# A turned tile stored in four scattered pieces and loaded whole, in a one-core transformer block

## The chip, the cores and the metric

The kernel runs on one core of a Trainium2 chip. The core has a matrix engine (TensorE, PE in the profile, with its weight loads as PEld), a vector engine (DVE), a scalar engine (ACT), a general engine (POOL), a queue engine (SP) and 16 DMA engines that move data between DRAM and the on-chip memory of 128 partitions (SBUF). The metric is the time of one launch in device microseconds, lower being better; the median of several runs is compared.

## The reference

One block over 256 tokens of width 2048, in float32: a gated FFN of width 5632, a mixer of two branches (a state-space scan, S5, and a gated spatial unit, SGU), and a second gated FFN, each with an RMS norm ahead and a residual around it.

```python
def swiglu_ffn(h, w_gate, w_up, w_down):
    return (jax.nn.silu(h @ w_gate) * (h @ w_up)) @ w_down

h = rms_norm(x, ffn1_norm[i])
x = x + 0.5 * swiglu_ffn(h, ffn1_w_gate[i], ffn1_w_up[i], ffn1_w_down[i])
h = rms_norm(x, mix_norm[i])
proj = h @ w_in[i]
y_a = s5_mixer(proj[..., :S5_WIDTH], ...)
y_b = sgu_mixer(proj[..., S5_WIDTH:], ...)
g_a, g_b = jnp.split(jax.nn.sigmoid(h @ w_gate[i] + b_gate[i]), 2, axis=-1)
x = x + (g_a * (y_a @ w_branch_a[i]) + g_b * (y_b @ w_branch_b[i])) @ w_out[i]
h = rms_norm(x, ffn2_norm[i])
x = x + 0.5 * swiglu_ffn(h, ffn2_w_gate[i], ffn2_w_up[i], ffn2_w_down[i])
return rms_norm(x, final_norm)
```

## The kernel before, in words

**Products.** Each weight and each activation is split into a high and a low part, and a product is three matmuls: high by high, high by low, low by high. `job` (L222) computes 256 tokens by 512 output columns: it runs `step` (L214) over the inner dimension in blocks of 128, six matmuls of 128x512 in each (three for either half of the tokens). The chunks of 128x2048 weights stand in one list in the order of their use. SP loads a chunk into `raw` (three buffers); ACT writes its high part `whi` (L148) and DVE its low part `wlo` (L149), three buffers of each; a chunk serves four steps. `take` (L195) calls `tick` (L176) once a step, and at a chunk's first step the chunk two further on is split. So the split of a chunk waits until TensorE is done with the one three before it.

**The order of the other work.** Every engine works in the order in which its instructions were written. Work that isn't matmuls is hung on ticks: `pend` holds what a finished product still needs and runs at the next tick, `at(n, fn)` runs fn n ticks later, and `fillers` are generators of which a step is run at some of the ticks. In the first FFN the filler is `s5_prepare` (L383), which computes the tables of S5, with many small transfers on POOL's queue and its arithmetic on DVE: `eb` and `bt` are loaded (L563, L565) and multiplied (L402), `ca` is stored as `stash_c` (L588) before the next `ca` is written.

**The FFN.** `ffn` (L331) runs in three groups of 4, 4 and 3 blocks of 512 hidden columns. For each block one job makes the gate product (`gate_evac`, SiLU into a tile `t`), one the up product (`up_evac`, L340, which multiplies into `t`, L347). The result lies tokens by columns and is wanted columns by tokens, split into high and low, in `gt`, for the down products after the group. Two ways lead there. The last block of a group is turned by TensorE, two ticks on (`turned`, L254: transposes `q`, L260, between the matmuls). The others, 3 + 3 + 2 in each FFN and 16 in all, go by `turned_dma` (L263): DVE transposes 32x32 blocks within 32 partitions (L266) into another buffer of `t`, POOL's queue carries the blocks to their places by way of a DRAM tile `turn`, into `w`, and 26 ticks after the call ACT and DVE split `w` into `gt` (L246, L247). `t` and `turn` have two buffers each, `w` one.

**POOL's queue.** POOL issues all of these transfers and the S5 ones, in the order written. A transfer that reads what another wrote is issued only when that one has landed, and POOL waits for it, so that all behind it on POOL waits too.

Of the kernel before, what the change touches and what calls it, by code (L numbers as in the profile page):

```python
# [9 lines left out]
F32 = mybir.dt.float32  # L10
# [8 lines left out]
P = 128  # L19
# [6 lines left out]
N = 512  # L26
# [24 lines left out]
def kernel(  # L51
# [31 lines left out]
    act, dve, pe, pool = nc.scalar, nc.vector, nc.tensor, nc.gpsimd  # L83
# [5 lines left out]
    dr = ctx.enter_context(tc.tile_pool(name="dr", bufs=1, space=DRAM))  # L89
# [79 lines left out]
    def at(delta, fn):  # L169
        hooks.setdefault(st["tick"] + delta, []).append(fn)  # L170
# [68 lines left out]
    def tmp():  # L239
        return ev.tile([P, 2, N], F32, tag="t", name="t", bufs=2)  # L240
# [22 lines left out]
    def turned_dma(src, pl, put, wait):  # L263
        tt = tmp()
        for h in range(2):
            dve.transpose(out=tt[:, h, :], in_=src[:, h, :])  # L266
        d = dr.tile([P, 2, N], F32, tag="turn", name="turn", bufs=2)
        pool.dma_start(out=d, in_=tt)  # L268
        dv = d.rearrange("(a j) h (k b i) -> a b j (h k) i", a=4, b=4, k=4)
        w = pl.tile([P, 2, 4, P], F32, tag="tw", name="w")  # L270
        for a in range(4):
            pool.dma_start(out=w.rearrange("p h k (a i) -> p a (h k) i", a=4)[:, a], in_=dv[a])  # L272

        def arrived():
            for h in range(2):
                put(slice(h * P, h * P + P), w[:, h])
        at(wait, arrived)
# [53 lines left out]
    def ffn(hT, gp, last_down, begin=None, rates=None):  # L331
# [8 lines left out]
        def up_evac(gt, j, n):  # L340
            def put(b, q):
                split2(gt[:, 4 * j + 2 * b:4 * j + 2 * b + 2], q)

            def evac(acc):
                s = state["g"]
                for h in range(2):
                    dve.scalar_tensor_tensor(out=s[:, h, :], in0=acc[:, h, :], scalar=rc(h), in1=s[:, h, :],  # L347
                                             op0=ALU.mult, op1=ALU.mult)
                if j < n - 1:
                    turned_dma(s, gp, lambda c, w: split2(gt[:, 4 * j:4 * j + 4], w, c), 26)  # L350
                else:
                    at(2, lambda: turned(s, 0, put))
            return evac
# [852 lines left out]
```

## Time and profile before

| what | value |
|---|---|
| median of 3 runs | 2039.59 us |
| lowest and highest | 2035.46 and 2049.26 us |
| the profiled execution | 2037.03 us |
| its span, first to last instruction | 2035.1 us |
| mean granted TensorE clock | 0.996 |
| busy: PE, DVE, ACT, POOL | 2010.9, 1146.0, 864.8, 216.8 us |
| POOL, 64 loads w<-turn (L272) | 134.5 us busy |
| POOL, 16 stores turn<-t (L268) | 9.3 us busy |
| DMA queue of SP, share of 16 engines | 56.6% |
| DMA queue of POOL, share of 16 engines | 10.1% |

A group of instructions is named by its line, engine, operation and what it writes and reads (`w<-turn`). In a timeline each row has the start in us from the span's beginning, how long the row's instructions took, engine, line, operation, tiles and count, and in brackets how long the engine had been idle and what ended that. For a transfer the time in the row is that of its issue; "DMA to landing" is the time from the issue until its data have arrived (least, median and most of the transfers asked for). In a list of waits stand the waiting engine and line, whom it waited for, the total in us, how often, and the longest.

### The profile page before, as it was taken

The numbers are of one execution on the slowest core, as the hardware profiler recorded it, in microseconds if no ns is written. First come the engines' busy times: TensorE is split into PE (matmuls) and PEld (weight loads), VectorE is DVE, ScalarE is ACT, GpSimd is POOL, SyncE is SP. The second block draws the span as 40 slices with busy tenths as digits, with TensorE's granted clock in tenths as the row PEclk, the third lists the DMA queues.
The fourth block names the chain that finished last, engine by engine and source line by source line (L and its number), as shares of the span: only waits on it lengthen the run. The fifth ranks groups of instructions, "written<-read, shape, count | busy, mean of one in ns | idle before, by whom it ended". The sixth has DMA issues, their size and how long they took to land.

```text
span 2035.1 us, 23133 instructions
## 1 busy us (share of the span) xinstructions
PE 2010.9 (99%) x9636; PEld 1662.4 (82%) x9636; DVE 1146.0 (56%) x1138; ACT 864.8 (42%) x709; POOL 216.8 (11%) x214
## 2 busy tenths in 40 slices
PE   9999999999999999989999999999999999999998
PEld 7887888887888888878888988888888888888886
DVE  5775565666664555546775565545554445544454
ACT  7543334444333455434345444443433343333343
POOL 0131002332012000010100000011100121000200
PEclk9999999999999999999999999999999999999999
DMA  8888678886668655547755544578855688555873
GB/s 313 223 230 220 241 233 226 234 236 200 218 211 223 195 197 196 204 171 263 242 198 209 205 175 177 180 211 216 224 201 191 201 208 224 199 198 203 212 214 124
DMA packets 78008, 429.75 MB, mean 211 GB/s; under 512 B 17696, under 2 KB 18352, under 8 KB 32080
## 3 DMA queue, kind: packets, MB, share of 16 engines
q1 hardware_dynamic: 53280, 378.56, 56.6%
q0 software_dynamic: 22176, 45.50, 10.1%
q10 hardware_dynamic: 2448, 4.22, 0.6%
q8 instruction: 75, 1.23, 0.3%
q14 instruction: 29, 0.24, 0.0%
HBM read 406.60 MB, written 20.84 MB: 210 GB/s over the span
## 4 chain that ended last, share of the span: by engine, by line
PE 90%; DMA 4%; issue 2%; DVE 1%; POOL 1%; ACT 1%; SPq 0%; ACTq 0%; POOLq 0%; DVEq 0%
PE acc L218 29%; PE acc L219 28%; PE acc L220 28%; DMA bt<-in_s5bt_dram 1%; PE q L260 1%; DMA raw<-in_w1s_dram 1%; DMA stash_c<-ca 1%; POOL w L272 1%; DMA raw<-in_w1u_dram 1%; DVE wlo L149 1%; ACT whi L148 1%; DMA stash_g<-gsb 0%; PE acc L236 0%; PE acc L235 0%; PE q L745 0%
## 5 line engine op out<-in xcount | busy, mean ns | idle before, releaser
L149 DVE TENSOR_TENSOR wlo<-raw,whi 128x2048 fp32r<-128x2048 f32 (+1 forms) x363 | 815.3, 2248 | 777.4 <-ACT whi L148 777.4
L148 ACT ACTIVATE whi<-raw 128x2048 fp32r<-128x2048 f32 (+1 forms) x363 | 682.6, 1882 | 916.9 <-PE acc L220 760.9
L218 PE MATMUL acc<-whi,h 128*128 128x512 f32 x1856 | 726.1, 391 | 0.9 <-ACT whi L148 0.9
L219 PE MATMUL acc<-wlo,h 128*128 128x512 f32 x1856 | 723.1, 390 | 1.2 <-DVE wlo L149 1.2
L220 PE MATMUL acc<-whi,h 128*128 128x512 f32 x1856 | 722.8, 389 | 0.0
L218 PEld LDWEIGHTS acc<-whi,h 128*128 128x128 f32 x1856 | 348.8, 188 | 74.1 <-ACT whi L148 1.3
L219 PEld LDWEIGHTS acc<-wlo,h 128*128 128x128 f32 x1856 | 348.8, 188 | 73.9 <-DVE wlo L149 2.3
L220 PEld LDWEIGHTS acc<-whi,h 128*128 128x128 f32 x1856 | 348.6, 188 | 72.8
L218 PE MATMUL acc<-whi,gt 128*128 128x512 f32 x680 | 266.9, 392 | 0.0
L219 PE MATMUL acc<-wlo,gt 128*128 128x512 f32 x680 | 265.6, 391 | 0.0
L220 PE MATMUL acc<-whi,gt 128*128 128x512 f32 x680 | 265.4, 390 | 0.0
L220 PEld LDWEIGHTS acc<-whi,gt 128*128 128x128 f32 x680 | 127.8, 188 | 27.6
L218 PEld LDWEIGHTS acc<-whi,gt 128*128 128x128 f32 x680 | 127.9, 188 | 27.1
L219 PEld LDWEIGHTS acc<-wlo,gt 128*128 128x128 f32 x680 | 127.9, 188 | 26.7
L272 POOL DMA_DIRECT2D w<-turn x64 | 134.5, 2105 | 134.3 <-issue 84.0
L268 POOL DMA_DIRECT2D turn<-t x16 | 9.3, 583 | 860.2 <-DVE t L266 860.2
L337 ACT ACTIVATE t<-acc,rc 128x512 f32<-128x512 f32 x44 | 27.9, 686 | 63.4 <-PE acc L220 63.4
L218 PE MATMUL acc<-whi,mT 128*128 128x512 f32 x128 | 50.2, 392 | 0.0
L220 PE MATMUL acc<-whi,mT 128*128 128x512 f32 x128 | 49.9, 389 | 0.0
L219 PE MATMUL acc<-wlo,mT 128*128 128x512 f32 x128 | 49.8, 389 | 0.0
L312 DVE SCALAR_TENSOR_TENSOR x_sb<-acc,x_sb 128x1024 f32<-128x1024 f32 x27 | 33.1, 1224 | 29.7 <-PE acc L220 29.7
L291 ACT ACTIVATE junk<-x_sb 128x512 bf16<-128x512 f32 x32 | 20.2, 631 | 57.2 <-DVE x_sb L312 51.9
(205 smaller groups left out, 1113.4 us busy)
## 6 DMA issues: line engine op xcount, KB each, us to landing
raw<-in_w1d_dram SPq DMA_DIRECT2D x44, 1024.0 KB, 5.1
raw<-in_w2g_dram SPq DMA_DIRECT2D x44, 1024.0 KB, 4.9
raw<-in_w2u_dram SPq DMA_DIRECT2D x44, 1024.0 KB, 5.3
raw<-in_w2d_dram SPq DMA_DIRECT2D x44, 1024.0 KB, 4.8
raw<-in_w1g_dram SPq DMA_DIRECT2D x40, 1024.0 KB, 5.7
raw<-in_w1u_dram SPq DMA_DIRECT2D x40, 1024.0 KB, 5.9
raw<-in_w_in_dram SPq DMA_DIRECT2D x24, 1024.0 KB, 4.8
raw<-in_w_gb_dram SPq DMA_DIRECT2D x16, 1024.0 KB, 5.0
```

The costliest lines, as they stand in the source:

```text
L148: act.activation(out=hi[:, s], in_=r[:, s], func=AF.Copy)
L149: dve.tensor_tensor(out=lo[:, s], in0=r[:, s], in1=f(hi[:, s]), op=ALU.subtract)
L218: pe.matmul(acc[:, h, :], lhsT=lhs[:, k, 0, t], rhs=hi, start=first, stop=False)
L219: pe.matmul(acc[:, h, :], lhsT=lhs[:, k, 0, t], rhs=lo, start=False, stop=False)
L220: pe.matmul(acc[:, h, :], lhsT=lhs[:, k, 1, t], rhs=hi, start=False, stop=last)
L260: pe.transpose(q[:, i, h * P:h * P + P], src[:, h, c:c + P], ident)
L268: pool.dma_start(out=d, in_=tt)
L272: pool.dma_start(out=w.rearrange("p h k (a i) -> p a (h k) i", a=4)[:, a], in_=dv[a])
L291: act.activation(out=j, in_=x_sb[:, h, m * N:m * N + N], func=AF.Square, accum_out=ssq[:, h, m:m + 1])
L312: dve.scalar_tensor_tensor(out=xs, in0=acc, scalar=scale, in1=xs, op0=ALU.mult, op1=ALU.add)
L337: act.activation(out=s[:, h, :], in_=acc[:, h, :], func=AF.Silu, scale=rc(h))
```

## The change

The rearrangement moves from the loads to the stores. Before, one store writes the transposed tile to DRAM as it lies, 128 rows of 4 KB, and four loads, one for each block of 32 rows, each fetch 1024 pieces of 128 bytes (32 numbers) and put them into all 128 partitions. After it, four stores, one for each 32 partitions of the tile, write 1024 pieces of 128 bytes each to their places in DRAM, and one load fetches 128 rows of 4 KB as they lie. `turn` has another shape and the same size; what arrives in `w` is the same.

```diff
         for h in range(2):
             dve.transpose(out=tt[:, h, :], in_=src[:, h, :])
-        d = dr.tile([P, 2, N], F32, tag="turn", name="turn", bufs=2)
-        pool.dma_start(out=d, in_=tt)
-        dv = d.rearrange("(a j) h (k b i) -> a b j (h k) i", a=4, b=4, k=4)
+        d = dr.tile([4, 32, 2, 4, P], F32, tag="turn", name="turn", bufs=2)
+        dv = d.rearrange("b j h k (a i) -> a j (h k) b i", a=4)
+        for a in range(4):
+            pool.dma_start(out=dv[a], in_=tt[32 * a:32 * a + 32].rearrange("j h (k b i) -> j (h k) b i", k=4, b=4))
         w = pl.tile([P, 2, 4, P], F32, tag="tw", name="w")
-        for a in range(4):
-            pool.dma_start(out=w.rearrange("p h k (a i) -> p a (h k) i", a=4)[:, a], in_=dv[a])
+        pool.dma_start(out=w.rearrange("p h k t -> p (h k t)"), in_=d.rearrange("b j h k t -> (b j) (h k t)"))
```

Only POOL's instructions differ. The first place is POOL at the third call, which stands at 143 us in the profile, with the loads of `eb` and `bt` behind it. In brackets are the counters that a row waits for: DVE_49 and Activation_49 count what DVE and ACT have done, DMASW0 to DMASW7 the landings of POOL's transfers, which take the eight counters in turn. Before:

```order
L268 DMA turn_1199<-t_1196 128x1024 [waits DMASW1_49,DVE_49]
L272 DMA w_1201<-turn_1199 128x8x32 [waits DMASW3_49,DMASW2_49,DMASW4_49,DMASW1_49,Activation_49]
L272 DMA w_1201<-turn_1199 128x8x32 x2
L272 DMA w_1201<-turn_1199 128x8x32 [waits DMASW5_49]
L563 DMA eb_1306<-stash_e_84 128x1x512 [waits DMASW7_49,DMASW6_49,DVE_49]
L563 DMA eb_1306<-stash_e_84 128x1x512 [waits DMASW0_49]
L565 DMA bt_1309<-in_s5bt_dram 128x2x512
```

And the same place on POOL after the change:

```order
L270 DMA turn_1199<-t_1196 256x4x32 [waits DVE_49]
L270 DMA turn_1199<-t_1196 256x4x32 x2
L270 DMA turn_1199<-t_1196 256x4x32 [waits DMASW4_49]
L272 DMA w_1204<-turn_1199 128x1024 [waits DMASW3_49,DMASW4_49,DMASW2_49,DMASW5_49,DMASW1_49,Activation_49]
L563 DMA eb_1306<-stash_e_84 128x1x512 [waits DMASW7_49,DMASW6_49,DVE_49]
L563 DMA eb_1306<-stash_e_84 128x1x512 [waits DMASW0_49]
L565 DMA bt_1309<-in_s5bt_dram 128x2x512
```

The wait for landed stores (counters 1 to 4) has moved from the second of the five transfers to the last, right ahead of `eb` and `bt`, and now stands for four stores instead of one.

The second place is POOL at the sixth call, at 419 us in the profile, with the store of `ca` and the small transfers of `gsb` behind it, as the difference between the two programs:

```order
 L622 DMA stash_t<-tt 128x512
 L556 DMA par<-in_s5bc_dram 128x4x128
-L268 DMA turn<-t 128x1024
-L272 DMA w<-turn 128x8x32 x4
+L270 DMA turn<-t 256x4x32 x4
+L272 DMA w<-turn 128x1024
 L588 DMA stash_c<-ca 128x1280
 L614 DMA stash_g<-gsb 16x1024
```

`stash_c` stood behind the issue of four loads and now stands behind the landing of four stores.

## The prediction

> **What bounds the kernel now.** I read the engines' shares first, then TensorE's waits, then a table of stretches cut where TensorE is idle, and last the timelines of POOL, DVE and ACT there. The columns of the stretches are: bounds, length, then the busy time (instructions) of PE, PEld, DVE, ACT and POOL, the granted clock, the DMA share and GB/s.
>
> ```profile
> PE q L260 <- DVE t L347: 5.3, 4, 3.9
> 180.00:196.00 16.00, 11.88 (x50) 9.51 (x49) 11.62 (x14) 4.09 (x5) 1.78 (x3) 0.89 0.55 194
> 196.00:456.00 260.00, 260.00 (x1209) 213.51 (x1208) 152.18 (x124) 109.18 (x91) 51.07 (x57) 1.00 0.79 233
> 456.00:470.00 14.00, 12.83 (x60) 10.22 (x59) 11.36 (x13) 5.47 (x5) 5.35 (x10) 1.00 0.64 202
> 864.00:885.00 21.00, 15.19 (x64) 12.26 (x63) 7.47 (x14) 4.98 (x4) 1.46 (x2) 0.84 0.33 119
> 885.00:2026.00 1141.00, 1140.23 (x5699) 945.78 (x5697) 618.31 (x439) 470.77 (x355) 95.74 (x83) 1.00 0.65 204
> 140.34 0.39 PE L219 MATMUL acc<-wlo,h 128*128 128x512 f32 x1
> 140.56 0.39 PE L220 MATMUL acc<-whi,h 128*128 128x512 f32 x1
> ```
>
> TensorE is the bound almost everywhere: from 196 to 456 us it has no idle time, from 885 to 2026 it has 0.8 us, although half of the 16 turned tiles pass there. It is idle in three places in mid program: 16.00 - 11.88 = 4.1 us near 186, 1.2 us near 462, and 5.8 us near 867, where no turned tile is under way. At the first the granted clock is 0.89 over 16 us, another 16 x 0.11 = 1.8 us. So the change can give back at most 4.1 + 1.8 + 1.2 = 7.1 us of 2035, and can cost time wherever it lets TensorE wait. Matmuls start 0.22 to 0.23 us apart (140.34, 140.56), so a weight chunk of 24 matmuls takes 24 x 0.226 = 5.4 us.
>
> **The change, part by part.** Before, a turned tile leaves as one store, and four loads fetch it. The rows are from the call at 1351.84, where nothing else uses POOL; the landing lines belong to the first and the fourth load, and the last row is ACT reading the tile.
>
> ```profile
> 1351.84 0.60 POOL L268 DMA_DIRECT2D turn<-t  x1 [270.66 <-DVE t L266]
> 1355.49 6.36 POOL L272 DMA_DIRECT2D w<-turn  x3 [3.04 <-DMA turn<-t]
> 1366.65 2.09 POOL L272 DMA_DIRECT2D w<-turn  x1 [4.80 <-issue]
> ...
> DMA to landing us min/median/max: 10.8/10.8/10.8
> ...
> DMA to landing us min/median/max: 16.4/16.4/16.4
> ...
> 1384.96 1.14 ACT L246 ACTIVATE gt<-w 128x512 fp32r<-128x512 f32 x2
> 1387.01 1.92 ACT L148 ACTIVATE whi<-raw 128x2048 fp32r<-128x2048 f32 x1 [0.91 <-PE acc L220]
> ```
>
> The four loads need 1366.65 + 16.4 - 1355.49 = 27.6 us, that is 6.9 us each, though POOL spends 2.1 us on each; the fourth is issued 0.4 us after the first has landed (1355.49 + 10.8 = 1366.3). The tile is complete 31.2 us after the store was issued, and is read at 33.1: 1.9 us to spare.
>
> Removed: the wide store, 0.6 us of POOL and 3.6 us until the first load starts. Added: four stores, each of 1024 pieces of 128 bytes, as many and as long as a load had, but written to DRAM in pieces where the loads read DRAM in pieces. POOL writes out as many pieces as before, so I take 2.1 us for each issue, beside other work. Their time to landing is the one unknown price. The nearest rows are the loads (same pieces, other direction) and the four stash_e stores of 32 KB, 128 pieces of 256 bytes each (same direction), which stood right behind a load:
>
> ```profile
> 118.23 2.10 POOL L272 DMA_DIRECT2D w<-turn  x1 [6.78 <-issue]
> 124.24 2.22 POOL L512 DMA_DIRECT2D stash_e<-em  x4 [3.91 <-DVE em L402]
> ...
> DMA to landing us min/median/max: 14.5/14.5/14.5
> ...
> DMA to landing us min/median/max: 9.2/9.2/9.3
> ```
>
> The first landing line is the load's, the second that of the small stores. The load landed at 118.23 + 14.5 = 132.7, the first small store at 124.24 + 9.2 = 133.4, the fourth, issued about 125.9, at 135.2. So 384 pieces took 1.8 us, about POOL's own pace of issue (0.56 us each): at most 4.8 us for 1024 pieces. Lower end of the price: POOL's 2.1 us for each store. Upper end: twice the loads' 6.9 us, since nothing in the trace writes 128-byte pieces. I take the loads' price, 27.6 us for four: the piece size and the count are the same, and the written row stands below it, not above.
>
> The Trainium skill speaks against the change here ("DMA: Bandwidth & Descriptors", Specifications): below 512 bytes a transfer falls short of line rate because the DMA engine reads, modifies and writes. By that rule as it stands stores and loads of 128 bytes are both slow, and the sum stays; taken as a rule for DRAM writes alone, it leads to the last rival below. The stash_e rows, at 256 bytes, show no such charge.
>
> Added too: one wide load, 512 KB in rows of 4 KB, which waits on POOL for all four stores. Loads of that size:
>
> ```profile
> vt<-stash_v POOLq DMA_DIRECT2D x4, 512.0 KB, 6.0
> tab<-stash_w POOLq DMA_DIRECT2D x4, 512.0 KB, 4.9
> ```
>
> So 5 to 6 us. The tile is then complete 27.6 + 0.4 + 5.5 = 33.5 us after the first store is issued, against 31.2: 0.4 us after ACT's usual 33.1. What covers it: the split that follows stands until 1387.01 for TensorE's release, 0.9 us after the reads end, and weights are split two chunks ahead, 10.8 us less 1.9 (ACT) and 2.3 (DVE) for the split, 6.6 us. A tile may be 7.5 us late before TensorE runs dry. Price of the later tile: 0. Without that cover each of the 16 calls would cost what exceeds it.
>
> The stage buffer t is held for 28 us instead of 3; its buffer is next written by the next call's transpose, two jobs of 16 steps on, 2 x 16 x 6 x 0.226 = 43 us. Price 0.
>
> The rest is what stands behind the call in POOL's queue, and only in the first FFN, where the preparation of the S5 tables runs beside it. Before, POOL was free once the fourth load was issued, and what followed queued in the DMA engines; now POOL itself stands until the stores have landed.
>
> ```profile
> 143.20 0.58 POOL L268 DMA_DIRECT2D turn<-t  x1 [16.74 <-DVE t L266]
> 146.79 6.31 POOL L272 DMA_DIRECT2D w<-turn  x3 [3.01 <-DMA turn<-t]
> 158.33 2.10 POOL L272 DMA_DIRECT2D w<-turn  x1 [5.24 <-issue]
> 160.43 1.21 POOL L563 DMA_DIRECT2D eb<-stash_e  x2
> 161.62 0.76 POOL L565 DMA_DIRECT2D bt<-in_s5bt_dram  x1
> 194.22 0.58 POOL L573 DMA_DIRECT2D stash_v<-vt  x1 [31.84 <-DVE vt L402]
> 196.02 0.77 POOL L565 DMA_DIRECT2D bt<-in_s5bt_dram  x1
> ...
> DMA to landing us min/median/max: 16.8/16.8/16.8
> ...
> DMA to landing us min/median/max: 9.8/9.8/9.8
> ...
> 184.25 1.29 DVE L402 TENSOR_TENSOR m<-eb,bt 128x512 f32<-128x512 f32 x2 [3.43 <-DMA bt<-in_s5bt_dram]
> 189.00 1.40 DVE L347 SCALAR_TENSOR_TENSOR t<-acc,rc,t 128x512 f32<-128x512 f32 x2
> ```
>
> Place one, the call at 143.20. The landing lines are those of the fourth load and of the second bt. The first bt landed at 184.2, as DVE's wait shows; DVE stood 3.4 us for it, the gate product t came late, and TensorE waited at its transposes (q): the 4.1 us. Now: four loads ran from 146.79 to 158.33 + 16.8 = 175.1, 28.3 us, so the stores land at 143.2 + 28.3 = 171.5; the wide load is issued at 171.9, eb and bt follow until 174.5. The same four sizes in a row were issued from 194.22, and the last, bt, landed at 196.02 + 9.8 = 205.8, 11.6 us on. So bt lands at 171.9 + 11.6 = 183.5: 0.7 us earlier. Term: -0.7 us. Bounds: -3.4 and the clock's 1.8 if the stores are cheaper, +2 if the wide load is the slower kind.
>
> ```profile
> 419.24 0.55 POOL L268 DMA_DIRECT2D turn<-t  x1
> 424.56 6.33 POOL L272 DMA_DIRECT2D w<-turn  x3 [4.76 <-DMA turn<-t]
> 438.86 2.09 POOL L272 DMA_DIRECT2D w<-turn  x1 [7.98 <-issue]
> 440.94 0.60 POOL L588 DMA_DIRECT2D stash_c<-ca  x1
> ...
> DMA to landing us min/median/max: 14.6/14.6/14.6
> ...
> DMA to landing us min/median/max: 15.6/15.6/15.6
> ...
> DMA to landing us min/median/max: 4.8/4.8/4.8
> ...
> 456.59 0.83 DVE L402 TENSOR_TENSOR ca<-m,m 128x640 f32<-128x640 f32 x1 [1.04 <-DMA stash_c<-ca]
> ```
>
> Place two, the call at 419.24. The landing lines are those of the fourth load, of stash_c and of the 512 KB store at 194.22. DVE overwrites ca only when stash_c has landed (440.94 + 15.6 = 456.5), and the next t follows: TensorE's 1.2 us. The loads took 438.86 + 14.6 - 424.56 = 28.9 us, and their first waited 4.8 us for a store that elsewhere took 3.0, so I add 1.7 for what lies ahead in the queue: stores landed at 419.24 + 28.9 + 1.7 = 449.8, wide load issued at 450.2, stash_c right behind it. At 194.22 the first 512 KB landed in 4.8 us and the next 1024 KB by 11.6, 6.8 us; 640 KB behind 512 KB take 4.8 + 6.8 x 640/1024 = 9.1 us, so stash_c lands at 450.2 + 9.1 = 459.3: +2.8 us. The call before it, at 372, ends its chain of small POOL transfers later in the same way, and this call follows that chain without a gap: +1.0 us, between 0 and 2.5. A wait grown from 1.2 to 5.0 us may also lower the clock as at 186: 0 to 1.8 us; I take 0.
>
> Sum: -0.7 + 2.8 + 1.0 = +3.1 us. The profiled execution took 2037.03 us (span 2035.1), so 2040.1, in round numbers 2040. It lay 2.6 us below the median 2039.59, so the same sum beside the median is 2042.7.
>
> **Rivals.**
> *The stores are cheaper than the loads.* The stash_e rows speak for it, with 4.8 us or less for 1024 pieces; against it, those were few, and of 256 bytes. Four stores then land after 19 us or less, bt and stash_c come over 8 us earlier, and both waits go: 3.4 + 1.8 + 1.0 = 6.2 us less, 2031. It can give no more, as TensorE is busy elsewhere.
>
> *The stores are dearer, and TensorE waits at every tile.* Mechanism: writes of 128 bytes to DRAM land later than reads, the wide load goes out later, and ACT, which works in order, stands at gt<-w ahead of the weight splits. It decides from 33.1 + 7.5 = 40.6 us after the first store on, that is when four stores take over 40.6 - 5.9 = 34.7 us, 1.26 times the loads. At 1.5 times (41.4 us) a call is 47.3 - 40.6 = 6.7 us too late, 16 calls 107 us, and with a lowered clock of up to 1.8 us at each 136: 2144 to 2173. At twice the price (55.2 us) 20.5 us a call, 328 us: 2365 or more. Against it: the stash_e rows. By the Trainium skill's rule above, read as one for DRAM writes alone, this is the case that comes, and 2365 stands against the 2040 by the rows.
>
> *It only trades places.* The same pieces cross the same DMA engines; 3.6 us before the loads become 5.9 us behind the stores, and both POOL places stay as they are: 2037. This lies within the forecast's own bounds.
>
> **How the numbers follow.** Forecast (loads' price, trading places with it): 0.56, its own range 2034 to 2046 by the bounds above. Cheaper stores: 0.24, 2029 to 2033. Dearer: 0.20, of which only a twentieth part lies below 2058, just past the tipping point. The range 2029 to 2058 then holds about 0.8. A measurement of this kernel tells about 1%, 20 us, from no change. Faster by that much is beyond the 7.1 us there are: 0.03 for what I have not seen. Slower by over 1%: nearly all of the dearer case, 0.19. Within 1%: 0.78.
>
> **What would show it.** In the profile after: L270 with 64 issues of about 2.1 us, the fourth of each call waiting for the first to land; L272 16 times, about 0.6 us, idle before it some 14 to 18 us for turn<-t. Landing of turn<-t near 10.8 to 16.4 us, as for the loads, says the price is right; under 6 us is the cheap case, over 21 the dear one. ACT gt<-w waiting for w about 0.5 us a call is the forecast; more than 7 us is the rival, and TensorE then has idle time after 1340. Near 186 the wait should stand at about 3.4 us and near 462 at some 5.0. I am wrong if weight loads land so late beside the stores that ACT waits for raw more than now and TensorE with it.

## The result and the profile after

| | before | after |
|---|---|---|
| median, 9 runs each | 2039.59 us | 2028.99 us |
| lowest and highest | 2034.53 and 2049.26 | 2028.22 and 2029.78 |
| profiled execution (span) | 2037.03 (2035.1) | 2029.23 (2027.3) |

After / before is 0.9946, with a 95% interval of 0.9931 to 0.9961: 10.6 us less, half a per cent. The runs also lie closer together: 1.6 us from lowest to highest instead of 14.7. The forecast was 2040 in a range of 2029 to 2058, so the median lies 0.01 us below its low end, and the sign of the movement was the other one.

From the page after: busy time by engine, packets, the queues of SP (q1) and POOL (q0), the shares of the chain that ended last, and the group of the scattering stores (busy us, mean ns, idle time before).

```profile
PE 2008.8 (99%) x9636; PEld 1660.9 (82%) x9636; DVE 1145.8 (57%) x1138; ACT 864.4 (43%) x709; POOL 144.9 (7%) x214
...
DMA packets 71865, 428.97 MB, mean 212 GB/s; under 512 B 11552, under 2 KB 12208, under 8 KB 25936
...
q1 hardware_dynamic: 53280, 378.56, 52.8%
q0 software_dynamic: 16032, 44.71, 7.7%
...
PE 97%; DVE 1%; DMA 1%; ACT 1%; issue 1%; SPq 0%; ACTq 0%
...
L270 POOL DMA_DIRECT2D turn<-t x64 | 63.5, 999 | 931.2 <-DVE t L266 931.2
```

The same lines of the page before:

```profile
DMA packets 78008, 429.75 MB, mean 211 GB/s; under 512 B 17696, under 2 KB 18352, under 8 KB 32080
...
q0 software_dynamic: 22176, 45.50, 10.1%
...
PE 90%; DMA 4%; issue 2%; DVE 1%; POOL 1%; ACT 1%; SPq 0%; ACTq 0%; POOLq 0%; DVEq 0%
```

POOL is busy 72 us less, and 1.0 us with each store where each load cost 2.1. The bytes are nearly the same, but POOL's queue has 22176 - 16032 = 6144 packets fewer, all of them small: 96 for each of the 64 loads that are gone. TensorE makes up 97% of the chain that ended last, where it was 90%.

TensorE's waits after (total us, times, longest), the two largest beside one of 1.4 us at the start of the program:

```profile
PE q L260 <- DVE u_all L934: 4.6, 1, 4.6
...
PE q L907 <- DVE u_all L934: 1.2, 1, 1.2
```

Both stood there before too, near 867. The waits for `t` (L347), 5.3 us in all before, are gone. The stretches after, with the columns of the prediction's table:

```profile
180.00:196.00 16.00, 16.00 (x76) 13.25 (x75) 11.58 (x11) 5.95 (x5) 2.57 (x4) 1.00 0.68 207
...
456.00:470.00 14.00, 14.00 (x67) 11.55 (x66) 9.42 (x12) 6.46 (x8) 0.00 (x0) 1.00 0.64 236
```

TensorE is busy without a gap at both places, at full clock. That is 4.1 us of idle time and 1.7 us of clock near 186, and 1.2 us near 462: 7.0 of the 7.8 us between the two spans.

How this comes about is seen at the third call. The timelines of POOL and of DVE after:

```profile
142.48 3.95 POOL L270 DMA_DIRECT2D turn<-t  x4 [16.14 <-DVE t L266]
153.40 0.56 POOL L272 DMA_DIRECT2D w<-turn  x1 [6.97 <-DMA turn<-t]
153.95 1.25 POOL L563 DMA_DIRECT2D eb<-stash_e  x2
155.19 0.76 POOL L565 DMA_DIRECT2D bt<-in_s5bt_dram  x1
...
177.57 1.28 DVE L402 TENSOR_TENSOR m<-eb,bt 128x512 f32<-128x512 f32 x2
...
183.13 1.40 DVE L347 SCALAR_TENSOR_TENSOR t<-acc,rc,t 128x512 f32<-128x512 f32 x2
```

And how long these transfers took from issue to landing (least, median, most), first the stores of this call, then its `bt`:

```profile
DMA to landing us min/median/max: 3.3/6.5/7.6
...
DMA to landing us min/median/max: 10.6/10.6/10.6
```

The four stores are issued 1 us apart, and POOL goes on 10.9 us after the first (153.40 - 142.48). The loads had taken 28 us here. `bt` lands at 155.19 + 10.6 = 165.8 instead of 184.2, 12 us before DVE comes to it, and `t` starts at 183.13 instead of 189.00. By page and timeline, then, four stores are far cheaper than the four loads they replace. What makes them so, and why that is worth microseconds at one call and nothing at others, the experiments ask.

### The profile page after: what moved, and what is told of

The parts are those of the page before. It is cut to its first block, busy times and chain, and to the rows that moved or that the text cites. A ratio compares the mean times of both kernels' runs of the same rounds, so it can differ in the third digit from the quotient of the medians.

```text
span 2027.3 us, 23118 instructions
## 1 busy us (share of the span) xinstructions
PE 2008.8 (99%) x9636; PEld 1660.9 (82%) x9636; DVE 1145.8 (57%) x1138; ACT 864.4 (43%) x709; POOL 144.9 (7%) x214
## 3 DMA queue, kind: packets, MB, share of 16 engines
q0 software_dynamic: 16032, 44.71, 7.7%
## 4 chain that ended last, share of the span: by engine, by line
PE 97%; DVE 1%; DMA 1%; ACT 1%; issue 1%; SPq 0%; ACTq 0%
PE acc L218 31%; PE acc L220 31%; PE acc L219 31%; PE q L260 1%; DMA raw<-in_w1s_dram 1%; ACT whi L148 0%; DVE wlo L149 0%; PE q L609 0%; PE acc L236 0%; PE acc L235 0%; PE acc L234 0%; PE q L745 0%; PE q L702 0%; DVE r L671 0%; PE acc L1099 0%
## 5 line engine op out<-in xcount | busy, mean ns | idle before, releaser
L270 POOL DMA_DIRECT2D turn<-t x64 | 63.5, 999 | 931.2 <-DVE t L266 931.2
L291 ACT ACTIVATE junk<-x_sb 128x512 bf16<-128x512 f32 x32 | 20.2, 630 | 56.9 <-DVE x_sb L312 51.6
L347 DVE SCALAR_TENSOR_TENSOR t<-acc,rc,t 128x512 f32<-128x512 f32 x44 | 30.9, 745 | 16.8 <-PE acc L220 16.8
```

Source lines behind the costliest of these rows:

```text
L270: pool.dma_start(out=dv[a], in_=tt[32 * a:32 * a + 32].rearrange("j h (k b i) -> j (h k) b i", k=4, b=4))
L291: act.activation(out=j, in_=x_sb[:, h, m * N:m * N + N], func=AF.Square, accum_out=ssq[:, h, m:m + 1])
```

## The experiments

These were the theories after the result. On the price: *direction* (pieces of 128 bytes are dear to fetch from DRAM and cheap to put there); *form* (the loads were dear by the shape of their access pattern). Each of the old loads runs over 128 partitions and, in DRAM, over a pattern whose first dimension is 4 (`b`); each new store takes 32 partitions, and its first dimension in DRAM is 32 (`j`) as the kernel writes it. (The program folds this 32 and the 8 behind it, which lie evenly, into one of 256: hence the `256x4x32` in its rows. The 4 of the old loads stays a 4 there.) On the gain: *place one*, by `bt`, by the tile `w` or by the weights coming late there; against it, a gain all over, from less traffic.

### Gathering again, in the stores' form

One wide store and four gathering loads, as before, but each load takes 32 partitions and begins with a dimension of 32 in DRAM.

```diff
-        dv = d.rearrange("(a j) h (k b i) -> a b j (h k) i", a=4, b=4, k=4)
+        dv = d.rearrange("(a j) h (k b i) -> b j (h k) a i", a=4, b=4, k=4)
...
-        for a in range(4):
-            pool.dma_start(out=w.rearrange("p h k (a i) -> p a (h k) i", a=4)[:, a], in_=dv[a])
+        for b in range(4):
+            pool.dma_start(out=w[32 * b:32 * b + 32].rearrange("j h k (a i) -> j (h k) a i", a=4), in_=dv[b])
```

> The wide store as before, and four gathering loads with the access pattern of the changed kernel's stores turned round: each load fills 32 partitions with 1024 pieces of 128 bytes. Theory direction (reading DRAM in small pieces is dear, writing it is not): the four loads take 25 to 29 us as before, the tile is complete about 31 us after the store, TensorE waits about 4 us near 186 us and about 1 us near 462, and the time is 2036 to 2043 us. Theory form (the pattern over 128 partitions with an outermost dimension of 4 is dear, in either direction): POOL spends 1.0 us instead of 2.1 on each load, the four take about 10 us, the tile is complete about 14 to 16 us after the store, neither wait is left, and the time is 2028 to 2031 us.

Measured: 2029.4 us, ratio to before 0.9956 (0.994 to 0.9971), as the theory of the form has it. The view of transfers (count, KB each, median us from issue to landing) of this kernel:

```profile
w<-turn POOLq DMA_DIRECT2D x64, 128.0 KB, 5.8
```

and of the kernel before:

```profile
w<-turn POOLq DMA_DIRECT2D x64, 128.0 KB, 14.8
```

Loads of the same bytes in the same number of 128-byte pieces, from the same kind of DRAM tile, land in 5.8 us instead of 14.8, and the whole gain is there. The direction is not the cause.

### Scattering, in the old loads' form

The changed kernel, its four stores each over 128 partitions, with a first dimension of 4 in DRAM: the mirror of the old loads.

```diff
-        dv = d.rearrange("b j h k (a i) -> a j (h k) b i", a=4)
-        for a in range(4):
-            pool.dma_start(out=dv[a], in_=tt[32 * a:32 * a + 32].rearrange("j h (k b i) -> j (h k) b i", k=4, b=4))
+        dv = d.rearrange("b j h k (a i) -> b a j (h k) i", a=4)
+        for b in range(4):
+            pool.dma_start(out=dv[b], in_=tt.rearrange("p h (k b i) -> p b (h k) i", k=4, b=4)[:, b])
```

> Four scattering stores and one wide load as in the changed kernel, but each store takes 1024 pieces of 128 bytes from all 128 partitions, with the access pattern of the loads before turned round (outermost dimension 4 on the DRAM side). Theory direction: POOL about 1 us for each store, the four land within about 10 us, 2028 to 2031 us. Theory form: POOL 2.1 us for each store, the fourth waits for the first to land, the four land after 25 to 29 us, the tile is complete after 31 to 35 us, and the time is 2036 to 2046 us.

Measured: 2034.07 us, ratio 0.9975 (0.9959 to 0.9991); the profiled run took 2040.84. Its transfers, and below its wait for `t`:

```profile
turn<-t POOLq DMA_DIRECT2D x64, 128.0 KB, 14.4
```

```profile
PE q L260 <- DVE t L347: 9.7, 4, 7.5
```

The stores are now as dear as the loads were, POOL's issue costs 131.5 us for the 64, and the 6144 small packets are back (17697 under 512 bytes). In this execution TensorE waits for `t` again. The form costs the same in both directions.

The time itself missed the 2036 to 2046 that was expected for the form: the median lies 5 us below the 2039.16 of before beside it. The twelve runs go from 2029.96, as fast as the changed kernel, to 2040.84, which is the one profiled. So the price of the transfers is shown, but how much of it reaches the time differs from run to run, and why it is less in most runs here stays open.

### 128 partitions without the dimension of 4

Does a transfer suffer from spanning all 128 partitions, or from the 4? Here the tile passes by four stores in the cheap form and four loads of 128 partitions each whose first dimension in DRAM is 128 too, once with the pieces 256 bytes apart and once adjacent.

```diff
+        d = dr.tile([4, 4, 32, 8, 64], F32, tag="turn", name="turn", bufs=2)
...
+            pool.dma_start(out=d[a].rearrange("b j k i -> j k b i")[:, :, :, 0:32],
+                           in_=tt[32 * a:32 * a + 32].rearrange("j h (k b i) -> j (h k) b i", k=4, b=4))
...
+            pool.dma_start(out=w.rearrange("p h k (a i) -> p a (h k) i", a=4)[:, a],
+                           in_=d[a].rearrange("b j k i -> (b j) k i")[:, :, 0:32])
```

> Both sides rearranged, to take the pattern of the loads before apart: four cheap scattering stores as in the changed kernel, then four loads of 1024 pieces of 128 bytes over all 128 partitions, whose DRAM side has no outermost dimension of 4 any more, but pieces 256 bytes apart, so that neither side of a load is whole. Theory outermost 4 (that dimension made the loads before dear): 1.0 us of POOL for each load and about 10 us for the four. Theory whole side (a transfer is cheap when one of its sides is in whole rows, because only the other is then cut into pieces): 2.1 us of POOL each, the fourth waits for the first to land, and 24 to 29 us for the four.

> The same with the DRAM pieces next to each other, so that a load's DRAM side is whole and its SBUF side is 1024 pieces over 128 partitions. Both theories: about 1.0 to 1.3 us of POOL for each load and about 10 us for the four. If they take 24 to 29 us here too, both fall, and it is the 128 partitions with eight pieces each that are dear.

Measured, one run each: 2028.83 and 2029.14 us. The loads with the pieces apart:

```profile
w<-turn POOLq DMA_DIRECT2D x64, 128.0 KB, 6.4
```

128 partitions alone don't make a load dear. All forms side by side (busy us of POOL for the 64 transfers, median us to landing; the first dimension as the kernel writes it, the program folds 32 to 256 and 128 to 1024):

| transfers | first dimension in DRAM, partitions | POOL | landing |
|---|---|---|---|
| loads, before | 4, 128 | 134.5 | 14.8 |
| stores of the second experiment | 4, 128 | 131.5 | 14.4 |
| stores, after | 32, 32 | 63.5 | 5.8 |
| loads of the first experiment | 32, 32 | 62.9 | 5.8 |
| loads of the third, apart | 128, 128 | 56.8 | 6.4 |
| loads of the third, adjacent | 128, 128 | 56.9 | 6.7 |

The dear ones are those with the 4 in front. No run has a 4 in front over 32 partitions, or another small number there, so how the price goes with that number isn't measured. The Trainium skill has a rule of this form ("DMA: Bandwidth & Descriptors", in the section on why a DMA increments its semaphore by 16 and not by 1): a transfer is spread over the largest number of DMA engines, up to 16, that divides the first dimension above 1 of both sides. By it the dear forms ran on 4 engines and the others on 16. All six rows agree with it, also with the folded dimensions; that only 4 engines were at work the trace doesn't show, since it names no engine for a packet, and neither does it say what the 96 extra packets are.

### Where in the program the gain arises

The changed form in some of the calls only; the others keep the old one.

```diff
+        n = turns[0]
+        turns[0] += 1
+        if n == 2:
...
```

The condition is `n >= 8` for the second FFN, `n == 2` for the third call (place one), `3 <= n <= 5` for calls 4 to 6 (place two among them).

> The changed form in the eight calls of the second FFN, the form before in the eight of the first. Theory queue (what counts is how long the S5 transfers behind a turned tile on POOL's queue are held up, which is so in the first FFN alone): no gain, 2036 to 2041 us, with TensorE's waits near 186 and 462 us still there. Rival, weights (the pieces hold up the weight loads in every call, and a part of a microsecond is won at each): half of the gain, about 2033 to 2035 us.

> The changed form in the third call alone (place one), the form before in the other 15. Theory places (the gain is what the waits near 186 and 462 us cost, and the first belongs to the third call): the wait near 186 and the lowered clock behind it are gone, the wait near 462 stays at 1 to 3 us, and the time is 2029 to 2033 us, most of the whole gain. Rival, stretch (the pieces of every call of the first FFN crowd the DMA engines, and each adds a share): a sixth to a third of the gain, 2036 to 2038 us.

> The changed form in the fourth, fifth and sixth call (place two), the form before elsewhere. Theory places: the wait near 462 is gone, that near 186 stays, with its changing size from run to run, and the time is 2035 to 2039 us, 1 to 4 us below before. Rival, stretch: half of the gain, 2032 to 2035 us.

| changed form in | median us | before beside it | ratio (95%) |
|---|---|---|---|
| the second FFN, 8 calls | 2039.68 | 2039.16 | 1.001 (0.9996 to 1.0025) |
| the third call alone | 2030.94 | 2039.23 | 0.9962 (0.9948 to 0.9976) |
| calls 4 to 6 | 2038.46 | 2039.23 | 0.9996 (0.9982 to 1.001) |

The third call alone brings 8.3 us, about four fifths of the gain. Eight calls of the second FFN bring nothing, and calls 4 to 6 nothing that can be told from nothing, though near 462 TensorE no longer waits there. So it is not a gain from less traffic: it arises where a late transfer reaches TensorE. The third call and calls 4 to 6 together make 9.1 of the 10.6 us; the rest is less than these intervals can tell, and the other calls of the first FFN had no run of their own.

The profile of the second-FFN kernel, whose first FFN is the old one, also shows that place one differs from run to run. Its wait:

```profile
PE q L260 <- DVE t L359: 9.4, 2, 9.3
```

There DVE went on with `bt` at 189.13, and TensorE's longest wait for `t` was 9.3 us, against 3.9 in the profiled execution of before.

### What is late at place one: bt moved out of POOL's queue

The kernel before, with `eb` and `bt` of the first group issued by ACT, so that they don't stand behind the gathering loads.

```diff
+            q = act if g == 0 else pool
...
-                pool.dma_start(out=eb[:, i, :], in_=se[i, :, gw].unsqueeze(1).to_broadcast([8, 16, GP * 64]))
+                q.dma_start(out=eb[:, i, :], in_=se[i, :, gw].unsqueeze(1).to_broadcast([8, 16, GP * 64]))
...
-            pool.dma_start(out=bt, in_=s5bt[:, :, gw])
+            q.dma_start(out=bt, in_=s5bt[:, :, gw])
```

> The turned tiles as before; only the loads of eb and bt of the first of the four S5 groups are issued from ACT's queue instead of POOL's, so that they no longer stand behind the four gathering loads of the third call. Theory queue: bt lands well before DVE wants it at 181 us, TensorE's wait of about 4 us near 186 and the lowered clock behind it are gone, the wait near 462 stays, and the time is 2029 to 2034 us. Rival, weights: the wait near 186 comes from the traffic of the pieces itself, and the time stays at 2036 to 2041 us.

Measured: 2037.23 us, ratio 0.9994 (0.9978 to 1.0009). Of that kernel the waits of ACT for weights from 150 to 200 us:

```profile
ACT whi L148 <- DMA raw<-in_w1u_dram: 7.0, 1, 7.0
...
ACT whi L148 <- DMA raw<-in_w1d_dram: 4.0, 1, 4.0
```

ACT's waits for weights in the kernel before, from 140 to 200 us (the changed kernel has none there):

```profile
ACT whi L148 <- DMA raw<-in_w1d_dram: 5.9, 2, 5.8
...
ACT whi L148 <- DMA raw<-in_w1u_dram: 3.2, 1, 3.2
```

And DVE's timeline with `bt` on ACT's queue:

```profile
181.04 1.29 DVE L247 TENSOR_TENSOR gt<-w,gt 128x512 fp32r<-128x512 f32 x2
182.25 1.29 DVE L402 TENSOR_TENSOR m<-eb,bt 128x512 f32<-128x512 f32 x2
...
186.99 1.40 DVE L347 SCALAR_TENSOR_TENSOR t<-acc,rc,t 128x512 f32<-128x512 f32 x2
```

DVE comes to `bt` without waiting, and yet `t` starts at 186.99, 3.9 us later than in the changed kernel, and TensorE waits 2.5 us. Now the weights are late: ACT stood 7.0 and 4.0 us for `raw`, so that it came to the tile `w` only at 178.71, when that had landed (157.96 + 19.2 = 177.2), and DVE split it at 181.04 instead of 176.36. Before, ACT had stood 9.1 us for `raw` here too, but `bt` came later still. The expectation that `bt` is the whole of it was missed. Since `bt`, the weights and the tile can each be late here, two more runs hold back one alone.

### One transfer late at a time

First a run that did not do what it was meant to: in the changed kernel `eb` and `bt` of the first group stand four steps later in the program.

```diff
+             early = 4 if g == 0 else 0
+             for _ in range(early):
+                 yield
...
```

> The changed kernel, with the loads of eb and bt of the first S5 group issued about 18 us later (four of the five filler steps between them and their use now stand ahead of them). The turned tile's pieces are then long through, so the DMA engines are no more crowded than in the changed kernel, and only bt is late, as it was before. Theory bt (DVE, which works in order, stands for bt, and TensorE for what DVE has behind it): DVE waits 3 to 6 us for bt, TensorE 3 to 6 us near 186 with a lowered clock behind it, 2033 to 2038 us. Rival, crowding (the wait before came from weights and tile held up on the DMA engines, bt's lateness being a bystander): no wait near 186, 2028 to 2030 us.

Measured: 2029.51 us, ratio 0.9948 (0.9933 to 0.9963). `bt` was issued at 154.51, no later than in the changed kernel (155.19): POOL has no work between, and its order alone does not hold a transfer back. The run tells nothing about a late `bt`.

So POOL was held by a chain of small copies between a scratch tile and DRAM, each waiting for the last. Seven of them ahead of `eb` and `bt` make only these late; six of them, behind `bt` and ahead of the wide load, make only the tile late. Both are the changed kernel otherwise, but for DVE filling the scratch tile once. The first of the two edits:

```diff
+            if g == 0:
...
+                for n in range(7):
+                    pool.dma_start(**(dict(out=ht, in_=hd) if n % 2 else dict(out=hd, in_=ht)))
```

> Changed kernel; in the third call seven small copies of 16 KB, each waiting for the one before, stand on POOL between the wide load and the eb and bt loads of the first group, so that bt alone is late and nothing crowds the transfers. By the spacing of the stores in the changed kernel (about 3 us from issue to landing) they hold POOL some 18 us: bt should land near 182 to 187 instead of 165.8 (184.2 before). Theory A (bt's lateness made the wait near 186): DVE waits for bt for 3 us or more, TensorE waits for t L347 near 186 again, and 3 to 8 us of the gain are lost: 2032 to 2037. Theory B (the crowding of the tile and the weights made it): DVE may wait for bt, but it catches up, and the time stays at 2028 to 2031.

> Changed kernel; in the third call the eb and bt loads are issued ahead of the wide load, and six small copies between them hold the wide load some 15 us, so that the turned tile w alone is late: it should land near 175 to 180 instead of 157.5 (175.1 before), and bt earlier than 165. Theory B1 (the late tile holds DVE up): DVE or ACT waits for w at the tile's four products and TensorE waits for t L347 near 186: 2031 to 2034. Theory B2 (the weight loads' lateness, not the tile's): no wait of TensorE near 186, 2028 to 2030.

Measured: with `bt` late 2041.11 us, ratio 1.0008 (0.9991 to 1.0024); with the tile late 2036.94 us, ratio 0.998 (0.9962 to 0.9998). DVE's timeline with `bt` late:

```profile
176.00 1.29 DVE L247 TENSOR_TENSOR gt<-w,gt 128x512 fp32r<-128x512 f32 x2
188.81 1.29 DVE L402 TENSOR_TENSOR m<-eb,bt 128x512 f32<-128x512 f32 x2 [11.51 <-DMA bt<-in_s5bt_dram]
...
193.55 1.40 DVE L347 SCALAR_TENSOR_TENSOR t<-acc,rc,t 128x512 f32<-128x512 f32 x2
```

and with the tile late:

```profile
182.98 1.29 DVE L247 TENSOR_TENSOR gt<-w,gt 128x512 fp32r<-128x512 f32 x2 [6.82 <-ACT gt L246]
184.19 1.28 DVE L409 TENSOR_TENSOR m<-eb,bt 128x512 f32<-128x512 f32 x2
...
188.92 1.40 DVE L354 SCALAR_TENSOR_TENSOR t<-acc,rc,t 128x512 f32<-128x512 f32 x2
```

`bt` alone late gives the whole gain back, and the tile alone late some 8 of the 10.6 us, while ACT waits for no weights from 150 to 200 us in either. Both took longer than was expected (2032 to 2037 and 2031 to 2034): the copies held more back than the kernel before did, `bt` to 188.8 instead of 184.2 and the tile to 177.02 + 5.3 = 182.3 instead of 175.1. So the runs show what a late `bt` or tile does, not the size of either in the kernel before, where the tile landed 2.1 us ahead of ACT's reading it (177.20). The theory that DVE would catch up with a late `bt` is refuted, and so is the one that only the weights' lateness counts. Whichever is late, it holds DVE, which works in order, ahead of `t`. Put together, the start of `t` (L347; the line moves with the edits), what held DVE before it, and TensorE's longest wait for it in the profiled run of each kernel:

| kernel | what is late | t starts at | TensorE waits |
|---|---|---|---|
| after | nothing | 183.13 | 0 |
| bt issued by ACT | weights | 186.99 | 2.5 |
| tile held | tile | 188.92 | 4.2 |
| before | weights, then bt | 189.00 | 3.9 |
| calls 4 to 6 only | weights, then bt | 189.04 | 4.4 |
| scattering in the old form | weights and tile, then bt | 192.06 | 7.5 |
| bt held | bt | 193.55 | 8.9 |
| second FFN only | weights and tile, then bt | 193.87 | 9.3 |

Start less wait lies between 184.5 and 185.1 in all that wait. That is the point from which it costs: in the changed kernel `t` has some 1.4 us to spare (184.5 - 183.13), and in these runs every microsecond beyond is paid in full.

### The wait that is left

The changed kernel, with the transposes and the start of S5 near 860 three ticks later, to see whether the 4.6 and 1.2 us there can go too.

```diff
-             at(1, lambda: turned(t, 0, put))
+             at(4, lambda: turned(t, 0, put))
...
-     pend.append(lambda: at(2, start_s5))
+     pend.append(lambda: at(5, start_s5))
```

> The changed kernel, with the one wait of TensorE that neither kernel touches, 5.8 us near 860, met at its place: the transposes of the S5 input are hung 4 ticks after their product instead of 1, and the start of the S5 branch 5 instead of 2. There the transposes stand in TensorE's queue ahead of matmuls that could run, and wait for a PSUM buffer that DVE frees only after a weight split. Theory: the wait shrinks from 5.8 to 0 to 2 us, the lowered clock behind it (half speed for 6.8 us) goes with it, and the time is 2019 to 2025 us, below both kernels. Rival: the S5 branch, started 4 us later, is waited for at its end, and the time stays within 2 us of 2029.

Measured: 2023.31 us (2022.3 to 2024.25), ratio to before 0.9918 (0.9902 to 0.9934): faster than both kernels. The stretches of the changed kernel,

```profile
860.00:865.00 5.00, 0.40 (x4) 0.19 (x3) 3.23 (x3) 1.44 (x1) 0.00 (x1) 0.97 0.14 16
865.00:872.00 7.00, 5.79 (x20) 4.77 (x20) 3.10 (x10) 0.00 (x0) 1.46 (x2) 0.53 0.58 217
```

and of this one:

```profile
860.00:865.00 5.00, 4.74 (x24) 3.71 (x24) 3.57 (x7) 1.72 (x2) 0.00 (x0) 1.00 0.09 13
865.00:872.00 7.00, 6.69 (x33) 5.48 (x34) 4.83 (x9) 1.59 (x1) 1.46 (x2) 1.00 0.75 248
```

Idle time there falls from 5.8 to 0.6 us, and the clock, at half in the second row, stays full, worth 7 x 0.47 = 3.3 us. Some 2 us come back later, where TensorE's wait for `y` (L671) grows from 0.7 to 2.8 us. 5.2 + 3.3 - 2.1 = 6.4, the difference of the two spans (2027.3 and 2020.9).

## Why the prediction was wrong

**The step that failed is the price of the four stores.** It was named the one unknown, and set at the loads' 27.6 us because "the piece size and the count are the same". They are, and so are the costs of both directions; but by the six forms what set the loads' price was a third property, the dimension of 4 in front of their pattern, and the change takes that away along with the gathering. It was in the diff to be read: the old `dv[a]` begins with `b`, the new one with `j`. Measured at the third call: 10.9 us from the first issue to the release of the wide load. POOL's 2.1 us for an issue was wrong for the same reason: it is 1.0. The prediction's own nearest row in the stores' direction, `stash_e` with at most 4.8 us for as many pieces, was the better neighbour (11 us for four is 2.7 each), and was set aside.

For place one the second experiment bears out that it was the price, and not what was built on it. There the stores do cost what the loads did, and the wide load is issued 172.36 - 143.92 = 28.4 us after the first store, where the sum had 28.7; `bt` is there at 187.3, where it had 183.5. The time of 2040 it does not bear out: the median is 2034.07, at the low end of the forecast's own 2034 to 2046.

**The rival of cheaper stores had the outcome.** It had both waits gone and a time of 2031, at a chance of 0.24. Its reason, the direction, was not the cause, as the first experiment shows: that it came true was in this part luck.

**The step "at most 7.1 us" held for the profiled execution and not for the median.** 7.0 us near 186 and 462 came back of 7.8. As a time it was nearly right: 2037.03 - 7.1 = 2029.9, and the median is 2028.99. As a gain it was too small: the profiled execution of before lay 2.6 us below its median, and place one has no fixed size: 4.1 us of waiting there, 9.4 in the execution of the second-FFN kernel, which runs the same code there and took 2042.0 us, with the lowered clock longer as well. That the median of before holds more of this wait than the profiled execution is a conclusion from these two; no execution at the median was profiled. A low end of 2029 left less than 1 us below 2029.9 for all that the rows did not show.

**Place one was the right place, its reading incomplete.** The prediction took the path from `bt` through DVE to `t` and the transposes, and the run with `bt` held confirms each link of it. It also took `bt` for the only late one: where `bt` comes in time and the dear loads stay, the weights are still late, and 2.5 us of waiting remain. The term of -0.7 us became -4.1 and -1.7.

**Place two went the other way.** For `stash_c` the prediction had +2.8 and +1.0; by the profile after, it was issued at 423.18 and landed 8.4 us later, at 431.6 instead of 456.5, and the 1.2 us are gone. In the medians this is within the noise (0.9996).

**What was right.** TensorE bounds the rest: eight calls in the second FFN are worth nothing (1.001). The wide load lands in a median of 4.3 us, against 5 to 6. That the tile may come earlier or later at the other calls without a price holds too: in the call at 1344.28 it is complete 1355.08 + 4.8 - 1344.28 = 15.6 us after the first store, against 31.2 before, and nothing is won there. The rival of dearer stores did not come. For the 512-byte sentence of the Trainium skill that the prediction weighed ("DMA: Bandwidth & Descriptors", Specifications): in one form, stores and loads of 128-byte pieces both land in 5.8 us, so writing shows no charge of its own here. That small pieces cost something at all shows beside the wide load: 512 KB in rows of 4 KB land in 4.3 us, and a quarter of that, in 128-byte pieces, in 5.8.

## What to carry to other kernels

Before pricing a transfer by a neighbour's row, compare the whole access pattern on both sides: the first dimension of either, the partitions and the pieces, not bytes and piece size alone. For a wait that varies from run to run, work out the gain from the spread of the runs, not from the one execution profiled. And when several transfers crowd one place, hold back one at a time: here a late `bt` and late weights were each enough to cause the wait, so freeing `bt` alone won nothing.

## What the runs showed of the hardware

- A transfer of 1024 pieces of 128 bytes with a first dimension of 4 in DRAM, over 128 partitions, costs POOL 2.1 us to issue and lands in a median of 14 to 15 us; the same pieces with 32 or 128 in front (256 or 1024 in the program) cost 0.9 to 1.0 and land in 5.8 to 6.7. Each of the dear ones carries 96 more small packets than those with 32 over 32 partitions.
- Dear transfers go with late weights on SP's queue: where they ran at the third call, ACT stood for weights between 140 and 200 us, 9.1 to 11.0 us in the four profiles with dear loads and 5.5 us in the one with dear stores, and in no profile with a cheap form there. How the one delays the other no run shows.
- The clock falls to 0.50 after a wait of 3.9 us or more and stays full after one of 2.5. After the wait of 8.9 us the lowered clock alone cost 3.3 us: the stretch from 194 to 204 us has 0.67. The Trainium skill states this as a rule ("TensorE: Matmul & The Clock Gate", Part 1), half clock after an idle window of about 3.4 us, and these waits agree. In the same run the clock near 880 was low longer, after waits as long as always: 1.7 us more than in the changed kernel.
